# The first FFN's gate and product move to PSUM, preparation blocks are cut into four steps, and the first map loads change queue

## The chip, the cores and the metric

The kernel runs on one core of a Trainium2 chip. The core has TensorE (matmuls; PE, and PEld for its weight loads), VectorE (DVE), ScalarE (ACT), GpSimd (POOL) and SyncE (SP, which here only issues DMAs). SBUF is the on-chip memory of 128 partitions; PSUM is TensorE's output memory, in eight banks of 128 x 512 float32. The metric is the device time of one execution in microseconds (us); less is better.

## The reference

A decoder trunk of two layers over 512 positions of width 1024, all in float32. Layer 0 mixes positions by attention, layer 1 by a state-space recurrence (S5); each mixer is followed by a gated FFN with a causal convolution of width 3. Cut to the parts that matter here:

```python
def s5_ssm(h, w_in, a_re, a_im, log_dt, b_re, b_im, c_re, c_im, d_skip, w_glu, b_glu, w_o):
    lam_bar = jnp.exp(lam * dt)
    b_bar = ((lam_bar - 1) / lam)[..., None] * b_mat
    ...
def conv_ffn(h, w_up, conv_w, conv_b, w_down):
    up = h @ w_up
    up = lax.conv_general_dilated(up, conv_w[:, None, :], ...) + conv_b
    gate, val = jnp.split(up, 2, axis=-1)
    return (jax.nn.silu(gate) * val) @ w_down
...
    x = x + g1[:, None, :] * y
    h = modulate(rms_norm(x, norm_ffn[i]), sh2, sc2)
    x = x + g2[:, None, :] * conv_ffn(h, w_up[i], conv_w[i], conv_b[i], w_down[i])
```

The maps of the state-space layer (powers of `lam_bar`, `b_bar`, products with `c`) depend on weights alone. They are computed while the first FFN runs.

## The kernel before, in words

**Three matmuls for one.** Each float32 weight is split into a high part (ScalarE copy to a rounded type, L163) and a low part (VectorE subtraction, L164); the activations likewise. `mm3` then issues three matmuls, high by high, high by low, low by high (L169, L172, L173). Weights arrive by SP as 128 x 1024 tiles (`up_r`, `dn_r`, L161) into three raw buffers and five pairs of split buffers. `split_next` keeps the loads and splits ahead of use; `bg` puts rows of the conditioning matrix (`wg`, L195 and L196) in between.

**The FFN.** The 22 units of 128 hidden channels come in three groups of 8, 8 and 6 (`GROUPS`). A unit computes two up tiles (gate and value, each one PSUM bank of the six in pool `mm`; a second pool `aux` has two banks for statistics), and `unit_out` finishes it: `conv` for the gate (ScalarE L457, then two VectorE taps L459), Silu in place on ScalarE (L466), `conv` for the value, the product `gm` on VectorE (L469), and its split `gH` (ScalarE L473) and `gL` (VectorE L474). After each group the down projection adds that group's units into the residual: eight tiles `dn`, each over all units of the group. The first two tiles go over all but the last unit before the last unit is wanted. The first two units of an FFN, the head, are computed while the norm is still being applied.

**Order.** On ScalarE and VectorE, `follow` chains the FFN's instructions in the order written. Otherwise a scheduler orders each engine's instructions ahead of time from modelled durations; `keep_in_program_order` (in `held` and `pe_pin`) ties an instruction behind the one traced before it on its engine. Each engine, and SP's queue, then runs in that fixed order.

**The preparation.** `ssm_prep` is a generator. `pace` is called with 11.0 after each unit from the third on and with 5.4 after each down tile, and calls `step()` once for each `PACE` of credit; each call runs to the next `yield`. First come the exponentials and sines (VectorE, small), powers and rotation tables (`cmul`, six GpSimd instructions L870 to L875, stored by GpSimd's own DMA, L992). Then the tables' pool closes and eight blocks follow. A block computes `bl` (`cmul` of the loaded maps `lam` and `bt`), `cl` (six GpSimd instructions from `bc` and the powers) and `bd` (copies), stores `bl` to `sB` and `cl` to `sC`; `direct` makes sixteen matmuls `pk` from `bd` and `cl`, a ScalarE copy and a VectorE correction into `kz`, and eight stores to `sT`. `cl_out` and `direct` run one block late (`owe`). The loads `ball`, `lam`, `bt`, `bc` and all these stores were issued by SP (L1006, L1022, L1025), most of them through `held`. The state-space stage reads `sB`, `sR`, `sT` and `sC` back after the FFN.

Of the kernel before, what the change touches and what calls it, by code (L numbers as in the profile page):

```python
# [16 lines left out]
P = 128  # L17
T = 512
# [21 lines left out]
NIDLE = (7, 4, 4)  # L40
USTG = (6, 7)
BGU = 2
PACE = 12.0
NHOLD = 2
APIN = 7
FILL = (4, 7, 10, 14)
# [44 lines left out]
def _trunk(ctx, tc, I, out, tap):  # L91
# [47 lines left out]
    def follow(eng, fn):  # L139
        with tc.issue_after(line[eng].ins) if eng in line else ExitStack():  # L140
            line[eng] = fn()
        return line[eng]
# [281 lines left out]
    def ffn(l, R, prep=None, last=None, hook=lambda: None):  # L424
# [4 lines left out]
        with ExitStack() as fc:  # L429
# [33 lines left out]
            def unit_out(i, j, pss, nxt=lambda: None):  # L463
                cg = conv(i, 0, pss[0])
                nxt()
                follow("S", lambda: S.activation(cg, cg, AF.Silu))  # L466
                cv = conv(i, 1, pss[1])
                m = fp.tile([P, T], F32, tag="gm", bufs=1, name="gm")
                follow("V", lambda: V.tensor_tensor(m, cg, cv, ALU.mult))  # L469
                nxt()  # L470
                gh = fp.tile([P, T], F32R, tag=f"gH{j}", name=f"gH{i}")
                gl = fp.tile([P, T], F32R, tag=f"gL{j}", name=f"gL{i}")
                follow("S", lambda: S.activation(gh, m, AF.Copy))  # L473
                follow("V", lambda: V.tensor_tensor(gl, m, gh.bitcast(F32), ALU.subtract))  # L474
                return gh, gl
# [389 lines left out]
    def ssm_prep(fc):  # L865
# [3 lines left out]
        def cmul(orr, oi, ar, ai, br, bi, t1, t2, e=E):  # L869
            e.tensor_tensor(t1, ar, br, ALU.mult)  # L870
            e.tensor_tensor(t2, ai, bi, ALU.mult)
            e.tensor_tensor(orr, t1, t2, ALU.subtract)
            e.tensor_tensor(t1, ar, bi, ALU.mult)
            e.tensor_tensor(t2, ai, br, ALU.mult)
            e.tensor_tensor(oi, t1, t2, ALU.add)  # L875
# [4 lines left out]
        def gen():  # L880
# [29 lines left out]
            V.tensor_tensor(ph, are, dt, ALU.mult)  # L910
            expo(mag, ph)
            yield

            V.tensor_tensor(ph, aim, dt, ALU.mult)
            NA = 9
# [41 lines left out]
            V.tensor_tensor(fi, t1, t2, ALU.subtract)  # L957
            V.tensor_tensor(fi, fi, den, ALU.mult)
            yield

            lf = pt_.tile([P, 2, 8, NPAIR], F32, tag="lf", name="lf")
            lt1, lt2 = (pt_.tile([P, 8, NPAIR], F32, tag=g, name=g) for g in ("lt1", "lt2"))
            f0, f1 = (f.rearrange("p (o q) -> p o q", o=1).to_broadcast([P, 8, NPAIR]) for f in (fr, fi))
            cmul(lf[:, 0, ::-1, :], lf[:, 1, ::-1, :], pw[:, 0, :8, :], pw[:, 1, :8, :], f0, f1, lt1, lt2)
            yield

            def lf_out():
# [9 lines left out]
            for hb in range(2):  # L977
                ps_ = slice(hb * HP, (hb + 1) * HP)
                tb = pt_.tile([P, 2, HP, NC], F32, tag="tb", name="tb")
                tt = pt_.tile([P, 2, HP, 32], F32, tag="tt", name="tt")  # L980
                E.memset(tb[:, 0, :, 0:1], 1.0)
                E.memset(tb[:, 1, :, 0:1], 0.0)
                for q in range(6):
                    n = 1 << q
                    e0, e1 = bcast(co[:, 3 + q, ps_], n), bcast(si[:, 3 + q, ps_], n)
                    cmul(tb[:, 0, :, n:2 * n], tb[:, 1, :, n:2 * n], tb[:, 0, :, :n], tb[:, 1, :, :n], e0, e1, tt[:, 0, :, :n], tt[:, 1, :, :n])
                    if q > 3:
                        yield
                    if hb == 0 and q == 4:
                        lf_out()  # L990
                for ri in range(2):
                    G.dma_start(sR[hb * 4:(hb + 1) * 4, :, ri, :].rearrange("b p n -> p b n"), tb[:, ri].rearrange("p (b q) c -> p b (q c)", b=4))  # L992
# [10 lines left out]
            bb = pb.tile([P, 2, NPAIR, 16], F32, tag="bb", name="bb")  # L1003
            ball = pb.tile([P, 2, NPAIR, 16], F32, tag="bl", name="ball")
            for ri in range(2):
                SP.dma_start(ball[:, ri].rearrange("p a b -> p (a b)"), I[("b_re", "b_im")[ri]])  # L1006

            def v3(t):
                return t[:, :512].rearrange("p (q o) -> p q o", o=16)
# [3 lines left out]
            def direct(bi, bd, cl):  # L1013
                pk = bank(aux, f"pk{bi}")
                for ri in range(2):
                    for q in range(4):
                        pe_pin(PE.matmul(pk[q * 32:(q + 1) * 32, :P], bd[:, ri, q, :], cl[:, ri, q, 0:8, :].rearrange("p a h -> p (a h)"), start=ri == 0, stop=ri == 1))
                kz = kza[:, bi % 2, :]
                S.activation(kz[:, 112:], pk[:, :P], AF.Copy)
                V.scalar_tensor_tensor(kz[:, 112:128], delta, sm("d_skip", bi, 1), kz[:, 112:128], ALU.mult, ALU.add)  # L1020
                for j in range(8):
                    SP.dma_start(sT[bi].rearrange("(h j) g c -> j g h c", j=8)[j], kz[:, 112 - 16 * j:240 - 16 * j])  # L1022

            def held(out, in_):
                tc.keep_in_program_order(SP.dma_start(out, in_))  # L1025

            def load_bl(bi):
                lam = pb.tile([P, 2, 512], F32, tag="lam", name="lam")
                bt = pb.tile([P, 2, 512], F32, tag="bt", name="bt")
                cs = slice(bi * 512, (bi + 1) * 512)  # L1030
                for ri in range(2):
                    held(lam[:, ri, :], sL[ri, :, cs].rearrange("(o j) x -> o j x", o=1).to_broadcast([16, 8, 512]))
                    held(bt[:, ri, :], I[("b_reT", "b_imT")[ri]][:, cs].rearrange("h (o x) -> h o x", o=1).to_broadcast([16, 8, 512]))
                return lam, bt

            def cl_out(bi, cl):
                for ri in range(2):
                    for g2 in range(2):
                        held(sC[bi, ri * 64:ri * 64 + 64].rearrange("n (q g) c -> g n q c", g=2)[g2],
                             cl[g2 * 64:g2 * 64 + 64, ri, :, 1:, :].rearrange("n q a h -> n q (a h)"))  # L1040
# [3 lines left out]
            nxt = load_bl(0)  # L1044
            for bi in range(8):
                qs = slice(bi * 4, bi * 4 + 4)
                if owe:
                    cl_out(bi - 1, owe[2])
                bc = pb.tile([P, 2, 4, 16], F32, tag="bc", name="bc")
                for ri in range(2):  # L1050
                    held(bc[:, ri].rearrange("p a b -> p (a b)"), I[("c_re", "c_im")[ri]][:, bi * 64:(bi + 1) * 64])
                bl = pb.tile([P, 2, 512], F32, tag="bl", name="bl")
                lam, bt = nxt
                cmul(bl[:, 0], bl[:, 1], lam[:, 0], lam[:, 1], bt[:, 0], bt[:, 1], t1[:, :512], t2[:, :512])
                yield
                held(sB[bi].rearrange("p r n -> p (r n)"), bl.rearrange("p r n -> p (r n)"))
                if bi < 7:
                    nxt = load_bl(bi + 1)
                if owe:
                    direct(*owe)  # L1060
                cl = pb.tile([P, 2, 4, 9, 16], F32, tag="cl", name="cl")

                def v4(t):
# [16 lines left out]
                for g2 in range(2):  # L1080
                    rr = slice(g2 * 64, g2 * 64 + 64)
                    E.tensor_copy(bd[rr, :, :, g2 * 16:g2 * 16 + 16], bb[rr, :, qs, :])
                owe = bi, bd, cl
                yield
            cl_out(7, owe[2])
            direct(*owe)
            tc2.close()

        g = gen()
# [406 lines left out]
```

## Time and profile before

| what | value |
|---|---|
| three runs | 1194.74, 1194.81, 1198.65 us (median 1194.81) |
| profiled execution | 1194.65 us |
| its span, first to last instruction | 1192.7 us |
| mean granted TensorE clock | 0.991 |
| busy: PE, DVE, ACT, POOL | 1168.8, 885.8, 563.7, 270.4 us |
| first FFN, first up matmul to last down stage's begin | 268.1 to 616.0 us |
| second FFN, the same | 820.2 to 1148.7 us |

Lines such as `L474 DVE TENSOR_TENSOR gL<-gm,gH 128x512 ... x8 | 13.3, 1663 | 0.0` name a source line, an engine, an operation, what it writes and reads, and its count; then busy time in us and mean ns of one; then the engine's idle time just before and what ended it. A line of waits reads: who <- whom: us in total, times, longest. A line of the timeline begins with the start and the length in us. "Granted clock" is the share of TensorE's full clock that the chip allowed in a stretch.

### The profile page before, as it was taken

The numbers are of one execution on the slowest core, as the hardware profiler recorded it, in microseconds if no ns is written. First come the engines' busy times: TensorE is split into PE (matmuls) and PEld (weight loads), VectorE is DVE, ScalarE is ACT, GpSimd is POOL, SyncE is SP. The second block draws the span as 40 slices with busy tenths as digits, with TensorE's granted clock in tenths as the row PEclk, the third lists the DMA queues.
The fourth block names the chain that finished last, engine by engine and source line by source line (L and its number), as shares of the span: only waits on it lengthen the run. The fifth ranks groups of instructions, "written<-read, shape, count | busy, mean of one in ns | idle before, by whom it ended". The sixth has DMA issues, their size and how long they took to land.

```text
span 1192.7 us, 16459 instructions
## 1 busy us (share of the span) xinstructions
PE 1168.8 (98%) x6218; PEld 964.4 (81%) x6218; DVE 885.8 (74%) x1312; ACT 563.7 (47%) x893; POOL 270.4 (23%) x245
## 2 busy tenths in 40 slices
PE   8999999999999999989999999999999999999997
PEld 6887677699787878768889887879888888888887
DVE  6978988565999489888868598787598467744555
ACT  6756667456443134413336577646554134422443
POOL 1000000000298899998710000000000000000003
PEclk8999999999999999989999999999999999999999
DMA  8875653231348567778755598762166437442222
GB/s 301 316 262 165 203 179 109 90 121 54 89 142 273 177 215 222 207 233 294 247 153 182 182 322 288 246 224 77 53 216 225 124 118 188 153 124 71 83 76 71
DMA packets 92002, 211.00 MB, mean 177 GB/s; under 512 B 19602, under 2 KB 37906, under 8 KB 91923
## 3 DMA queue, kind: packets, MB, share of 16 engines
q1 hardware_dynamic: 83026, 205.76, 53.9%
q10 hardware_dynamic: 8320, 2.10, 0.8%
q0 software_dynamic: 576, 2.10, 0.5%
q8 instruction: 48, 0.79, 0.3%
q14 instruction: 32, 0.25, 0.1%
HBM read 188.68 MB, written 21.24 MB: 176 GB/s over the span
## 4 chain that ended last, share of the span: by engine, by line
PE 70%; POOL 8%; DVE 8%; DMA 7%; ACT 3%; issue 2%; SPq 1%; POOLq 0%; ACTq 0%; DVEq 0%
PE up L169 9%; PE up L172 9%; PE up L173 9%; PE dn L172 5%; PE dn L169 5%; PE dn L173 5%; PE o L772 2%; DVE ca L459 1%; PE t L754 1%; PE k L169 1%; PE q L169 1%; PE wo L169 1%; PE q L172 1%; PE q L173 1%; PE wo L173 1%
## 5 line engine op out<-in xcount | busy, mean ns | idle before, releaser
L173 PE MATMUL up<-hH,up_l 128*128 128x512 f32 x640 | 249.3, 390 | 1.1 <-DVE up_l L164 1.1
L169 PE MATMUL up<-hH,up_h 128*128 128x512 f32 x640 | 249.5, 390 | 0.0
L172 PE MATMUL up<-hL,up_h 128*128 128x512 f32 x640 | 249.3, 390 | 0.0
L459 DVE SCALAR_TENSOR_TENSOR ca<-up,small,ca 128x511 f32<-128x511 f32 (+1 forms) x176 | 131.4, 746 | 84.2 <-ACT ca L457 81.4
L196 DVE SCALAR_TENSOR_TENSOR wg<-wg,cact 128x1024 f32<-128x1024 f32 x96 | 122.8, 1294 | 40.1 <-DMA wg<-in_w_modT_dram 39.9
L172 PE MATMUL dn<-gL,dn_h 128*128 128x512 f32 (+1 forms) x394 | 145.9, 370 | 3.4 <-DVE gL L474 3.4
L169 PE MATMUL dn<-gH,dn_h 128*128 128x512 f32 (+1 forms) x394 | 146.3, 372 | 2.1 <-ACT gH L473 2.1
L173 PE MATMUL dn<-gH,dn_l 128*128 128x512 f32 (+1 forms) x394 | 145.7, 370 | 0.0
L173 PEld LDWEIGHTS up<-hH,up_l 128*128 128x128 f32 x640 | 120.1, 188 | 26.9 <-DVE up_l L164 2.0
L169 PEld LDWEIGHTS up<-hH,up_h 128*128 128x128 f32 x640 | 120.1, 188 | 26.0 <-issue 1.2
L172 PEld LDWEIGHTS up<-hL,up_h 128*128 128x128 f32 x640 | 120.1, 188 | 24.4
L1368 POOL TENSOR_SCALAR xa<-x,Anorm_out 128x256 f32<-128x256 f32 x7 | 5.7, 815 | 573.7 <-ACT dn_h L163 558.9
L163 ACT ACTIVATE up_h<-up_r 128x1024 fp32r<-128x1024 f32 x80 | 84.2, 1053 | 104.7 <-PE dn L172 48.0
L164 DVE TENSOR_TENSOR up_l<-up_r,up_h 128x1024 fp32r<-128x1024 f32 x80 | 121.9, 1524 | 10.1 <-ACT up_h L163 9.2
L457 ACT ACTIVATE ca<-up,small 128x512 f32<-128x512 f32 x88 | 67.7, 770 | 90.3 <-PE up L173 90.3
L172 PEld LDWEIGHTS dn<-gL,dn_h 128*128 128x128 f32 x394 | 75.1, 191 | 16.3 <-DVE gL L474 4.0
L169 PEld LDWEIGHTS dn<-gH,dn_h 128*128 128x128 f32 x394 | 75.0, 190 | 15.9 <-ACT gH L473 3.0
L173 PEld LDWEIGHTS dn<-gH,dn_l 128*128 128x128 f32 x394 | 75.0, 190 | 12.4
L353 DVE SCALAR_TENSOR_TENSOR x<-dn,mod,x 128x512 f32<-128x512 f32 (+1 forms) x55 | 37.3, 679 | 61.6 <-PE dn L173 61.6
L163 ACT ACTIVATE dn_h<-dn_r 128x1024 fp32r<-128x1024 f32 (+1 forms) x48 | 46.7, 981 | 55.9 <-PE dn L172 28.0
L466 ACT ACTIVATE ca<-ca 128x512 f32<-128x512 f32 x44 | 27.8, 632 | 91.7 <-DVE ca L459 89.9
L164 DVE TENSOR_TENSOR dn_l<-dn_r,dn_h 128x1024 fp32r<-128x1024 f32 (+1 forms) x48 | 62.8, 1308 | 8.3 <-ACT dn_h L163 8.1
(324 smaller groups left out, 2352.2 us busy)
## 6 DMA issues: line engine op xcount, KB each, us to landing
wg<-in_w_modT_dram SPq DMA_DIRECT2D x96, 512.0 KB
up_r<-in_w_up_dram SPq DMA_DIRECT2D x80, 512.0 KB
dn_r<-in_w_down_dram SPq DMA_DIRECT2D x32, 512.0 KB
wgs<-in_w_modT_dram SPq DMA_DIRECT2D x16, 512.0 KB
dn_r<-in_w_down_dram SPq DMA_DIRECT2D x16, 384.0 KB
wv_r<-in_w_v_dram SPq DMA_DIRECT2D x8, 512.0 KB
wk_r<-in_w_qk_dram SPq DMA_DIRECT2D x8, 512.0 KB
wq_r<-in_w_qk_dram SPq DMA_DIRECT2D x8, 512.0 KB
```

Of the source, the lines that this page charges most:

```text
L163: order("S", lambda: S.activation(wh[:, :n], raw[:, :n], AF.Copy))
L164: pin["split"] = order("V", lambda: V.tensor_tensor(wl[:, :n], raw[:, :n], wh[:, :n].bitcast(F32), ALU.subtract))
L169: ins = PE.matmul(ps, ah, bh, start=start, stop=False)
L172: PE.matmul(ps, ah, bl, start=False, stop=False)
L173: PE.matmul(ps, al, bh, start=False, stop=stop)
L196: mul = lambda: V.scalar_tensor_tensor(w, w, 1.0, cact, ALU.mult, ALU.mult, accum_out=raw[:, col:col + 1])
L353: add = lambda: V.scalar_tensor_tensor(xs, pv, gate, xs, ALU.mult, ALU.add)
L457: follow("S", lambda: S.activation(ca, ps, AF.Identity, bias=small[:, cb:cb + 1], scale=tapw[2]))
L459: follow("V", lambda: V.scalar_tensor_tensor(ca[:, q:], ps[:, :T - q], tapw[2 - q], ca[:, q:], ALU.mult, ALU.add))
L466: follow("S", lambda: S.activation(cg, cg, AF.Silu))
L754: ins = PE.transpose(pt[:, c:c + P], wts[pr][h2][i][:, j * P:(j + 1) * P], ident)
L772: ins = PE.matmul(po[pr][h2 * HD:(h2 + 1) * HD, j * P:], vn[:, j, hd:hd + HD], src, start=j == 0, stop=j == 3)
```

## The change

Four edits, all of them in the first FFN or in the preparation that runs beside it (`prep` is given for layer 0 alone).

1. `unit_out`: with `prep`, one PSUM bank `gm` a unit takes both the Silu's result and, in place, the product. Units 0 and 1 take it from `aux`, the others from `mm`. Before, the Silu was in place in SBUF and the product in an SBUF tile.
2. `PACE` is 6.0, not 12.0. The steps ahead of the blocks get a second, empty `yield`, so they keep their distance; a block has four steps: the product `bl`; the store of the block before's `cl`, its `direct` and the `bc` loads; `cl`, `bd` and half of the block before's `sT` stores; the store of `bl`, the next block's map loads and the other half of the `sT` stores.
3. The `sT` stores leave `direct`, become `t_out`, and go through `held`.
4. The two `ball` loads and the four map loads of block 0 are issued by GpSimd.

```diff
-PACE = 12.0
+PACE = 6.0
...
                 cg = conv(i, 0, pss[0])
                 nxt()
-                follow("S", lambda: S.activation(cg, cg, AF.Silu))
+
+                m = bank(aux if i < 2 else mm, "gm") if prep else fp.tile([P, T], F32, tag="gm", bufs=1, name="gm")
+                ga = m if prep else cg
+                follow("S", lambda: S.activation(ga, cg, AF.Silu))
                 cv = conv(i, 1, pss[1])
-                m = fp.tile([P, T], F32, tag="gm", bufs=1, name="gm")
-                follow("V", lambda: V.tensor_tensor(m, cg, cv, ALU.mult))
+                follow("V", lambda: V.tensor_tensor(m, ga, cv, ALU.mult))
...
             expo(mag, ph)
             yield
+            yield
...
             for ri in range(2):
-                SP.dma_start(ball[:, ri].rearrange("p a b -> p (a b)"), I[("b_re", "b_im")[ri]])
+                G.dma_start(ball[:, ri].rearrange("p a b -> p (a b)"), I[("b_re", "b_im")[ri]])
...
-                for j in range(8):
-                    SP.dma_start(sT[bi].rearrange("(h j) g c -> j g h c", j=8)[j], kz[:, 112 - 16 * j:240 - 16 * j])
+
+            def t_out(bi, js):
+                kz = kza[:, bi % 2, :]
+                for j in js:
+                    held(sT[bi].rearrange("(h j) g c -> j g h c", j=8)[j], kz[:, 112 - 16 * j:240 - 16 * j])
...
             def load_bl(bi):
+                put = held if bi else G.dma_start
...
-                    held(lam[:, ri, :], sL[ri, :, cs].rearrange("(o j) x -> o j x", o=1).to_broadcast([16, 8, 512]))
-                    held(bt[:, ri, :], I[("b_reT", "b_imT")[ri]][:, cs].rearrange("h (o x) -> h o x", o=1).to_broadcast([16, 8, 512]))
+                    put(lam[:, ri, :], sL[ri, :, cs].rearrange("(o j) x -> o j x", o=1).to_broadcast([16, 8, 512]))
+                    put(bt[:, ri, :], I[("b_reT", "b_imT")[ri]][:, cs].rearrange("h (o x) -> h o x", o=1).to_broadcast([16, 8, 512]))
...
             for bi in range(8):
                 qs = slice(bi * 4, bi * 4 + 4)
-                if owe:
-                    cl_out(bi - 1, owe[2])
-                bc = pb.tile([P, 2, 4, 16], F32, tag="bc", name="bc")
-                for ri in range(2):
-                    held(bc[:, ri].rearrange("p a b -> p (a b)"), I[("c_re", "c_im")[ri]][:, bi * 64:(bi + 1) * 64])
                 bl = pb.tile([P, 2, 512], F32, tag="bl", name="bl")
                 lam, bt = nxt
                 cmul(bl[:, 0], bl[:, 1], lam[:, 0], lam[:, 1], bt[:, 0], bt[:, 1], t1[:, :512], t2[:, :512])
                 yield
-                held(sB[bi].rearrange("p r n -> p (r n)"), bl.rearrange("p r n -> p (r n)"))
-                if bi < 7:
-                    nxt = load_bl(bi + 1)
                 if owe:
+                    cl_out(bi - 1, owe[2])
                     direct(*owe)
+                bc = pb.tile([P, 2, 4, 16], F32, tag="bc", name="bc")
+                for ri in range(2):
+                    held(bc[:, ri].rearrange("p a b -> p (a b)"), I[("c_re", "c_im")[ri]][:, bi * 64:(bi + 1) * 64])
+                yield
                 cl = pb.tile([P, 2, 4, 9, 16], F32, tag="cl", name="cl")
...
+                if owe:
+                    t_out(bi - 1, range(4))
                 owe = bi, bd, cl
+                yield
+                held(sB[bi].rearrange("p r n -> p (r n)"), bl.rearrange("p r n -> p (r n)"))
+                if bi < 7:
+                    nxt = load_bl(bi + 1)
+                if bi:
+                    t_out(bi - 1, range(4, 8))
                 yield
             cl_out(7, owe[2])
             direct(*owe)
+            t_out(7, range(8))
```

More of the change, by code (lines that the diff above doesn't have):

```diff
@@ L988, in gen @@
                         yield
+                        yield
                     if hb == 0 and q == 4:
@@ L1055, in gen @@
                 yield
-                held(sB[bi].rearrange("p r n -> p (r n)"), bl.rearrange("p r n -> p (r n)"))
-                if bi < 7:
-                    nxt = load_bl(bi + 1)
                 if owe:
+                    cl_out(bi - 1, owe[2])
                     direct(*owe)
+                bc = pb.tile([P, 2, 4, 16], F32, tag="bc", name="bc")
+                for ri in range(2):
+                    held(bc[:, ri].rearrange("p a b -> p (a b)"), I[("c_re", "c_im")[ri]][:, bi * 64:(bi + 1) * 64])
+                yield
                 cl = pb.tile([P, 2, 4, 9, 16], F32, tag="cl", name="cl")
@@ L1082, in gen @@
                     E.tensor_copy(bd[rr, :, :, g2 * 16:g2 * 16 + 16], bb[rr, :, qs, :])
+                if owe:
+                    t_out(bi - 1, range(4))
                 owe = bi, bd, cl
+                yield
+                held(sB[bi].rearrange("p r n -> p (r n)"), bl.rearrange("p r n -> p (r n)"))
[3 more added lines that the diff above has]
+                    t_out(bi - 1, range(4, 8))
                 yield
```

## The prediction

> **What bounds the kernel now.** I read the page first, then busy time by stretch, then TensorE's waits, then the instructions around each wait. The page says where the floor is.
>
> ```profile
> PE 1168.8 (98%) x6218; PEld 964.4 (81%) x6218; DVE 885.8 (74%) x1312; ACT 563.7 (47%) x893; POOL 270.4 (23%) x245
> ```
>
> TensorE is busy for 98% of the span, so no engine's total can shrink the time; only what TensorE loses can. The two FFNs are the same code on the same sizes, but only the first carries the state-space preparation, so the second is a ruler for the first. Below, busy time by stretch: first-group up, its down, second-group up, its down, third-group up, for layer 0 and then for layer 1. Columns: stretch, length, busy of PE, PEld, DVE, ACT, POOL, granted clock, DMA share and GB/s.
>
> ```profile
> 268.10:359.00 90.90, 90.00 (x469) 76.77 (x467) 76.89 (x175) 47.31 (x71) 37.67 (x57) 1.00 0.32 95
> 359.00:406.50 47.50, 45.80 (x195) 37.15 (x194) 33.96 (x38) 12.92 (x15) 37.38 (x46) 0.96 0.63 207
> 406.50:496.60 90.10, 89.85 (x434) 72.88 (x433) 78.18 (x69) 33.93 (x47) 86.92 (x60) 1.00 0.72 224
> 496.60:548.20 51.60, 47.75 (x225) 37.85 (x224) 39.02 (x37) 11.26 (x14) 49.99 (x33) 0.93 0.81 258
> 548.20:616.00 67.80, 67.80 (x337) 54.95 (x337) 57.76 (x60) 26.73 (x38) 42.48 (x26) 1.00 0.76 232
> 820.20:909.40 89.20, 89.20 (x465) 76.41 (x464) 70.38 (x114) 48.97 (x72) 0.00 (x0) 1.00 0.41 131
> 909.40:952.90 43.50, 43.50 (x193) 36.03 (x192) 22.66 (x26) 11.15 (x12) 0.00 (x0) 1.00 0.53 169
> 952.90:1039.90 87.00, 87.00 (x385) 72.06 (x384) 62.76 (x87) 35.29 (x45) 0.00 (x0) 1.00 0.56 152
> 1039.90:1083.50 43.60, 43.60 (x194) 36.08 (x194) 18.72 (x20) 10.63 (x11) 0.00 (x0) 1.00 0.38 119
> 1083.50:1148.70 65.20, 65.20 (x289) 54.01 (x288) 35.38 (x44) 25.30 (x33) 0.00 (x0) 1.00 0.26 74
> ...
> L1017 PE MATMUL pk<-cl,bd x128: 272/273/423, 439.2 to 604.8; 128*32 128x128 f32 x128
> ...
> 268.10:616.00 347.90, 0.60 (x4) 0.50 (x4) 0.58 (x1) 0.99 0.62 195
> ```
>
> Layer 0 is longer by 1.7, 4.0, 3.1, 8.0 and 2.6 us, 19.4 in all. Part of that is TensorE's own preparation work: eight groups of sixteen `pk` matmuls (the tile's row) and four `ptl` transposes of 0.60 us (the last row, busy time of that tile alone). Three `pk` groups fall in the third up stretch, which has no idle time, so one costs 2.6/3 = 0.87 us. Three more fall in the second up stretch and two in its down. That is 6.9 + 0.6 = 7.5 us of work; 19.4 - 7.5 = **11.9 us is loss**: 1.1 in the first up, 4.0 in the first down, 0.5 in the second up, 6.3 in the second down. The waits of TensorE and the clock tell how it is lost.
>
> ```profile
> PE dn L172 <- DVE gL L474: 3.4, 2, 2.7
> PE dn L169 <- ACT gH L473: 2.1, 2, 1.1
> PE up L173 <- DVE up_l L164: 1.1, 2, 0.9
> ...
> 368.70:375.30 6.60, 4.90 (x14) 3.64 (x14) 6.60 (x10) 3.69 (x4) 6.21 (x8) 0.74 0.79 241
> 506.20:515.30 9.10, 5.25 (x26) 3.32 (x26) 8.13 (x8) 2.75 (x3) 8.93 (x5) 0.62 0.70 215
> ```
>
> In each of the first two down stages TensorE reaches the product of the group's last unit before `gH` and `gL` are made: 1.0 + 0.7 us idle in the first, 1.1 + 2.7 in the second. After each wait the granted clock falls (0.74 and 0.62 over the two stretches), which makes 4.0 us out of 1.7 and 6.3 out of 3.8.
>
> **The change part by part.** *Gate and product in PSUM (22 units).* No instruction is added; Silu now writes a PSUM bank, the product reads bank and SBUF and writes the bank, and `gL` reads bank and SBUF. The rows are VectorE by form, first from 406 to 548 us with GpSimd running, then from 820 to 1000 without it.
>
> ```profile
> L474 DVE TENSOR_TENSOR gL<-gm,gH 128x512 fp32r<-128x512 f32 x8 | 13.3, 1663 | 0.0
> L459 DVE SCALAR_TENSOR_TENSOR ca<-up,small,ca 128x511 f32<-128x511 f32 x16 | 11.8, 738 | 0.0
> L469 DVE TENSOR_TENSOR gm<-ca,ca 128x512 f32<-128x512 f32 x8 | 9.9, 1244 | 0.2
> L164 DVE TENSOR_TENSOR up_l<-up_r,up_h 128x1024 fp32r<-128x1024 f32 x16 | 33.4, 2090 | 5.7 <-ACT up_h L163 5.7
> ...
> L164 DVE TENSOR_TENSOR up_l<-up_r,up_h 128x1024 fp32r<-128x1024 f32 x24 | 29.3, 1219 | 0.7 <-ACT up_h L163 0.2
> L459 DVE SCALAR_TENSOR_TENSOR ca<-up,small,ca 128x511 f32<-128x511 f32 x24 | 18.0, 748 | 24.6 <-ACT ca L457 24.6
> L469 DVE TENSOR_TENSOR gm<-ca,ca 128x512 f32<-128x512 f32 x12 | 8.3, 692 | 0.4
> L474 DVE TENSOR_TENSOR gL<-gm,gH 128x512 fp32r<-128x512 f32 x11 | 7.5, 686 | 1.4 <-ACT gH L473 1.4
> ```
>
> With GpSimd running, every operation on two SBUF tensors is stretched (`gL` 686 to 1663 ns, `gm` 692 to 1244, `up_l` 1219 to 2090); the convolution tap, one PSUM and one SBUF input, is not (748 and 738). So I take 0.75 us for both new operations. No row has VectorE writing PSUM: the ends are 0.69 us (nothing but the size counts) and today's 1.24 and 1.66 (nothing gained; a loss is excluded by nothing but the tap, which is nearest). Gain per unit 0.49 + 0.91 = 1.4 us of VectorE, about 11 us over the second group's eight units, worth only what the two waits return. Units 0 and 1 take their bank from the statistics' pool: the statistics and their broadcast have been read by then, since the head's operands are made from them, so this costs nothing; were it not free, ScalarE would stand at the Silu with the next unit's copies behind it.
>
> [...]
>
> First down stage. The queue of VectorE there, the ScalarE row that makes the last `gH`, and ScalarE's copy out of PSUM by form:
>
> ```profile
> 350.62 1.53 DVE L474 TENSOR_TENSOR gL<-gm,gH 128x512 fp32r<-128x512 f32 x1
> 353.76 1.52 DVE L459 SCALAR_TENSOR_TENSOR ca<-up,small,ca 128x511 f32<-128x511 f32 x2
> 358.68 2.20 DVE L469 TENSOR_TENSOR gm<-ca,ca 128x512 f32<-128x512 f32 x1
> ...
> 369.08 0.63 ACT L473 ACTIVATE gH<-gm 128x512 fp32r<-128x512 f32 x1 [1.05 <-DVE gm L469]
> ...
> L457 ACT ACTIVATE ca<-up,small 128x512 f32<-128x512 f32 x16 | 12.2, 762 | 0.0
> ```
>
> VectorE is busy for all 6.60 us around the wait, so what is cut earlier arrives there. The `gL` and the `gm` shown give back 0.78 + 1.45 = 2.2 us, more than the 1.7 that TensorE waited. ScalarE's `gH` takes 0.63 us from SBUF; its copy out of PSUM, with two pointers, 0.76, so 0.13 us each for `gH` and Silu is the worst, and they eat 0.3 of the 0.5 to spare. The whole **4.0 us** goes. Next late is then the `dn_l` split of the tile after, in the same queue.
>
> *Preparation blocks in four steps.* The second down stage, VectorE and ScalarE:
>
> ```profile
> 502.10 1.52 DVE L164 TENSOR_TENSOR dn_l<-dn_r,dn_h 128x1024 fp32r<-128x1024 f32 x1 [3.65 <-ACT dn_h L163]
> 505.09 1.59 DVE L469 TENSOR_TENSOR gm<-ca,ca 128x512 f32<-128x512 f32 x1
> 508.82 1.75 DVE L474 TENSOR_TENSOR gL<-gm,gH 128x512 fp32r<-128x512 f32 x1
> ...
> 501.00 1.06 ACT L163 ACTIVATE dn_h<-dn_r 128x1024 fp32r<-128x1024 f32 x1 [5.73 <-DMA dn_r<-in_w_down_dram]
> ...
> SPq L1025 <- POOL bl L875: 28.8, 7, 6.5
> SPq L1006 <- DMA sR<-tb: 18.0, 2, 15.6
> ...
> 489.98 0.33 SPq L1025 DMA_DIRECT2D sB<-bl  x1
> 493.01 1.01 SPq L161 DMA_DIRECT2D dn_r<-in_w_down_dram  x2
> ```
>
> PSUM alone gives 0.84 (`gm`) + 1.00 (`gL`) = 1.84 of the 3.8 us idle. The rest hangs on a load: ScalarE stands 5.73 us for `dn_r`, and the last unit's Silu and product stand behind it. That load was issued at 493.01, behind `sB` and four map loads; `sB` was held until GpSimd had finished `bl`, one of seven such holds of 28.8 us together, 6.5 at most. In the new order `sB` comes three steps of 6 us behind its product instead of one of 12, with the store of the previous `cl` behind the next product, and the eight `sT` stores in two lots a step or two behind their matmuls. If the 6.5 us go, `dn_h` can be some 5.7 us earlier and the 3.65 us of VectorE idle with it: 1.84 + 3.65 = 5.5, more than 3.8. Only 2.0 of the 3.65 are needed. I take **5.3 of 6.3 us**, keeping 1.0 for a load that is still somewhat late. What can be late next: GpSimd's next product, whose maps are now loaded one step ahead of it; TensorE meets that only in `pk`, after the product and `cl`.
>
> The count of steps and the pace balance: 24 steps of 12 were 288 credits, 47 of 6 are 282. The first content comes half a block (6 us) earlier, into the third unit. Its small VectorE operations surround the `up_l` wait of the first up stretch (1.1 us lost); it may go or double. I take 0, ends -1.1 and +1.1.
>
> *First loads by GpSimd.* Two `ball` and four map loads leave SP, where they were held up to 15.6 us for `sR` to land, with weights behind them. TensorE lost 0.5 us in the stretch that follows; I take **0.5 us** back. GpSimd pays for six issues:
>
> ```profile
> L992 POOL DMA_DIRECT2D sR<-tb x4 | 3.3, 816 | 0.6 <-POOL tb L875 0.6
> ```
>
> 6 x 0.82 = 4.9 us on its queue, hidden because the last `pk` (604.8) stands 11 us ahead of the third up's end (616.0) and only later stages read the stores.
>
> *Sum*: 4.0 + 5.3 + 0.5 = 9.8 us. The profiled execution took 1194.65 us (span 1192.7 and 1.95 around it), 0.16 under the median of 1194.81: 1194.65 - 9.8 = **1184.9 us**. All 11.9 us back would be 1182.8.
>
> **The rivals.** *The load stays late, PSUM works.* Then the second down keeps 2.0 us idle and its share of slow clock: 6.3 x 2.0/3.8 = 3.3 stays, gain 4.0 + 3.0 + 0.5 = 7.5, 1187.2 us. For it: GpSimd itself is what SP waits for, and it is busy 49.99 of 51.60 us there.
>
> *The queue waits in a new place.* The `sT` stores are now held in order and need `pk`, a ScalarE copy and a VectorE operation; a weight load behind one of them stalls ScalarE as `dn_r` did. If one wait of the second down's size returns, 4.0 + 0.5 or less is kept: 1190 to 1194.5 us, no change. For it: seven holds at present, and an order that was timed for instructions of other length. Against: each store is now further behind what it waits for.
>
> *Slower: the banks run out.* Each unit now takes three of six banks, so the banks of a unit come round after two units, not three. The up tile of unit 6 ended three tiles before 358.4, at 5.2 us each: 342.8; its taps (the row at 353.76) ended at 355.3, a lag of 12.5 us, and the bank is wanted after 3 x 5.2 = 15.6. From a lag of 15.6 on TensorE waits in the middle of up. One us over, on six units, at the 4.0/1.7 that an idle us costs with the clock: 6 x 2.35 = 14 us, against a gain then of at most 5: 1204 us. Against it: the new lengths shorten the lag.
>
> [...]
>
> **How the numbers follow.** Forecast 0.46 (1182.8 to 1187), late load 0.16, new place 0.23, starved issues 0.04, banks 0.11. A measurement of this kernel can tell about 0.5%, 6 us. Faster by more: 0.46 + 0.16 = 0.62; within: 0.27; slower: 0.11. The range goes from 1181.8 (all the loss back, and 1 us that another order in later stages may give) to 1194.8 (the whole of the new-place case), leaving out the banks and little else; the likeliest case alone spans 1182.8 to 1187.
>
> **What would show it.** `gm` and `gL` in layer 0 near 0.75 us throughout; `up_l` still near 2; the waits of `dn` on `gH` and `gL` gone and the clock 1.00 in both down stretches, which then last 43.5 and 45.3 us; SP's hold on `bl` well under 28.8 us. Wrong if VectorE writing PSUM is slow, if a wait on `up` or `dn` appears that ends with a tap (banks), or if an order shifted after 616 us moves the state-space stage, which I hold unchanged.

## The result, and the profile after

The changed kernel took 1199.11 us (median of 20 runs, 1196.94 to 1204.29) against 1194.28 us for the kernel before (20 runs). The ratio is **1.0046, with a 95% interval of 1.0033 to 1.0058**: a little slower, and outside the range of the prediction. The profiled execution has a span of 1196.0 us and a mean clock of 0.991. Busy time of the engines, kernel after:

```profile
PE 1167.7 (98%) x6218; PEld 965.4 (81%) x6218; DVE 853.3 (71%) x1312; ACT 564.4 (47%) x893; POOL 254.5 (21%) x251
```

VectorE has 32.5 us less to do and GpSimd 15.9, TensorE the same work as before. The time is not lost to more work.

First the view that the prediction used as its ruler: busy time by stretch, first FFN of the kernel after (first up, its down, second up, its down, third up; columns as before).

```profile
269.70:360.60 90.90, 90.28 (x469) 76.71 (x468) 76.68 (x176) 49.88 (x75) 37.96 (x59) 1.00 0.36 108
360.60:404.10 43.50, 43.50 (x194) 36.03 (x192) 35.67 (x43) 11.23 (x12) 35.55 (x45) 1.00 0.75 244
404.10:511.60 107.50, 92.44 (x450) 74.32 (x448) 59.03 (x65) 36.03 (x49) 93.89 (x76) 0.92 0.69 204
511.60:556.80 45.20, 45.20 (x229) 36.64 (x225) 36.75 (x39) 10.67 (x13) 38.50 (x25) 1.00 0.86 270
556.80:623.90 67.10, 67.10 (x324) 54.75 (x321) 45.71 (x55) 25.59 (x36) 32.60 (x22) 1.00 0.65 197
```

Against the rows of before (90.9, 47.5, 90.1, 51.6 and 67.8 us) the two downs gained 4.0 and 6.4 us and both run at clock 1.00, as forecast. The second up lost 17.4 us, and here lies the whole surprise: PE was busy for only 92.44 of 107.50 us. The five stages sum to 354.2 us against 347.9, 6.3 more; the medians differ by 4.8. TensorE's waits of this stretch of the program, kernel after (who <- whom: us in total, times, longest):

```profile
PE pk L1023 <- POOL cl L1083: 11.8, 1, 11.8
PE pk L1023 <- POOL cl L1086: 3.3, 1, 3.3
PE up L173 <- DVE up_l L164: 0.3, 1, 0.3
PE up L169 <- DVE ca L459: 0.3, 1, 0.3
```

All waits on `gH` and `gL` are gone. In their place stands one that the kernel before did not have: the first `pk` matmuls wait 15.1 us for GpSimd's `cl`. The instructions around it, on TensorE and then on GpSimd, kernel after:

```profile
414.75 0.39 PE L173 MATMUL up<-hH,up_l 128*128 128x512 f32 x1
426.92 0.65 PE L1023 MATMUL pk<-cl,bd 128*32 128x128 f32 x8 [11.78 <-POOL cl L1083]
430.86 0.66 PE L1023 MATMUL pk<-cl,bd 128*32 128x128 f32 x8 [3.28 <-POOL cl L1086]
431.44 0.80 PE L169 MATMUL up<-hH,up_h 128*128 128x512 f32 x1
```

```profile
425.47 1.39 POOL L1083 TENSOR_TENSOR cl<-t,t 128x576 f32<-128x576 f32 x1
...
429.41 1.40 POOL L1086 TENSOR_TENSOR cl<-t,t 128x576 f32<-128x576 f32 x1
```

TensorE stands in front of `pk` from 415.1 us, one unit into the second up. GpSimd finishes the two halves of `cl` at 426.86 and 430.81. The same two events in the kernel before, one row of each engine:

```profile
434.41 2.29 POOL L1078 TENSOR_TENSOR cl<-t,t 128x576 f32<-128x576 f32 x1
...
439.21 0.64 PE L1017 MATMUL pk<-cl,bd 128*32 128x128 f32 x16
```

There `cl` was ready at 436.70 and `pk` came at 439.21, three units into the up: 2.5 us to spare. So GpSimd is not late in the changed kernel, it is 5.9 us *earlier*. It is TensorE that comes to `pk` too early, by two units (48 up matmuls ahead of it in this stretch instead of 144).

The credits of the pace give the reason. Six units of 11.0 and eight down tiles of 5.4 make 109.2 at the begin of the second up; 120.2 stand after unit 8, 131.2 after unit 9 and 142.2 after unit 10. Block 0's `direct` was in the 11th step of 12, due at 132, and so came after unit 10. In the new division it is in the 20th step of 6, due at 120, and comes after unit 8. Twelve credits are about one unit; 131.2 against 132 made it two.

A second wait hides behind the first. SP's holds on `bl` and on `kz`, and SP's queue around the first of them, kernel after:

```profile
SPq L1034 <- POOL bl L877: 29.4, 2, 27.2
...
SPq L1034 <- DVE kz L1026: 2.1, 2, 1.7
```

```profile
395.34 0.33 SPq L195 DMA_DIRECT2D wg<-in_w_modT_dram  x1
422.96 0.33 SPq L1034 DMA_DIRECT2D sB<-bl  x1
...
426.20 0.53 SPq L161 DMA_DIRECT2D up_r<-in_w_up_dram  x1
```

Where seven holds of 6.5 us at most stood, there is one of 27.2. SP, no longer held by `ball`, ran on to block 0's `sB` at 395.7 and stood there until GpSimd had made `bl`; the next weight was issued at 426.20. TensorE was waiting for `cl` at the time, so this cost nothing more, as long as the other wait stood. Two runs below bear out that the moved loads brought it: with only edit 1 and the loads still on SP (e4) the longest hold on `bl` is 5.6 us, and with only the loads moved (e10) it is 25.4.

### The profile page after: what moved, and what is told of

The parts are those of the page before. It is cut to its first block, busy times and chain, and to the rows that moved or that the text cites. A ratio compares the mean times of both kernels' runs of the same rounds, so it can differ in the third digit from the quotient of the medians.

```text
span 1196.0 us, 16497 instructions
## 1 busy us (share of the span) xinstructions
PE 1167.7 (98%) x6218; PEld 965.4 (81%) x6218; DVE 853.3 (71%) x1312; ACT 564.4 (47%) x893; POOL 254.5 (21%) x251
## 4 chain that ended last, share of the span: by engine, by line
PE 82%; POOL 9%; DVE 5%; ACT 2%; issue 1%; DMA 1%; POOLq 0%; ACTq 0%; DVEq 0%
PE up L169 12%; PE up L172 11%; PE up L173 11%; PE dn L169 5%; PE dn L173 5%; PE dn L172 5%; PE o L774 2%; PE u L172 1%; PE t L756 1%; PE u L169 1%; PE u L173 1%; PE wo L169 1%; PE wo L173 1%; PE wo L172 1%; PE k L169 1%
## 5 line engine op out<-in xcount | busy, mean ns | idle before, releaser
L169 PEld LDWEIGHTS up<-hH,up_h 128*128 128x128 f32 x640 | 120.5, 188 | 26.7 <-issue 2.1
L164 DVE TENSOR_TENSOR up_l<-up_r,up_h 128x1024 fp32r<-128x1024 f32 x80 | 112.7, 1408 | 1.9 <-ACT up_h L163 1.0
L163 ACT ACTIVATE dn_h<-dn_r 128x1024 fp32r<-128x1024 f32 (+1 forms) x48 | 46.8, 982 | 44.9 <-PE dn L172 38.1
```

The source lines that it names most:

```text
L163: order("S", lambda: S.activation(wh[:, :n], raw[:, :n], AF.Copy))
L164: pin["split"] = order("V", lambda: V.tensor_tensor(wl[:, :n], raw[:, :n], wh[:, :n].bitcast(F32), ALU.subtract))
L169: ins = PE.matmul(ps, ah, bh, start=start, stop=False)
```

## Experiments

The medians of the kernel before lay between 1191.79 and 1194.69 us in the four sets of runs, so each kernel is given by its ratio to the runs beside it. Outside the first FFN, profiled executions of one and the same code differ by some us (the state-space stage from its first `u` matmul to the `wos` matmuls took 119 to 123 us over all kernels, before among them); the stages of the FFN are therefore read from the trace. Where an expectation counts up matmuls ahead of `pk`, the count begins 142 matmuls ahead of the second up.

**e1, two steps later.** Block 0's `pk`, with all of its `sT` stores, behind the store of block 1's `sB`; the other blocks unchanged.

```diff
-                    direct(*owe)
+                    if bi > 1:
+                        direct(*owe)
...
-                owe = bi, bd, cl
+                late, owe = owe, (bi, bd, cl)
...
+                if bi == 1:
+                    direct(*late)
```

> The changed kernel with block 0's sixteen pk matmuls (and its sT stores) written two steps later, at 132 credits, so that they follow unit 10 on TensorE as in the kernel before, not unit 8. Theory (place): the 15.1 us of TensorE waiting for GpSimd's cl of block 0 is the whole loss, and all other parts of the change gain: cl ends near 431 us, TensorE reaches pk near 436, no wait; the second up stretch falls from 107.5 to about 90 us, the kernel from 1199.1 to about 1181.7, 12.6 us under the kernel before. Rival (GpSimd late because of its own six DMA issues): the same here, as the place hides the lateness. Rival (the wait only moves, since TensorE's time was never the limit): 1190 or more, with a new wait of the same kind at pk1 or later.

Measured: 1187.65 us, ratio 0.9939 (0.9919 to 0.9960), 6.0 us above the time that the theory gave. The `pk` wait is gone and the second up takes 97.2 us, not 107.5. That the change is now faster than the kernel before shows the first wait as the main cause (10.3 of the 17.4 us). But 97.2 is not 90: the second wait has come into the open. Waits of TensorE, of SP, and ScalarE's row ahead of it, e1:

```profile
PE up L169 <- ACT up_h L163: 2.6, 1, 2.6
PE up L173 <- DVE up_l L164: 1.6, 2, 1.2
```

```profile
SPq L1034 <- POOL bl L877: 40.2, 5, 27.4
```

```profile
433.16 1.06 ACT L163 ACTIVATE up_h<-up_r 128x1024 fp32r<-128x1024 f32 x1 [17.02 <-DMA up_r<-in_w_up_dram]
```

SP's hold of 27.4 us keeps a weight back, ScalarE waits 17.02 us for it, and TensorE waits for 4.2 us of that.

**e2, one step later.** Only the `pk` of block 0, behind the making of block 1's `cl`.

> As e1, but one step later instead of two: pk of block 0 follows unit 9. Place: TensorE reaches it near 425.3, cl ends near 431, so it waits 5 to 6 us and loses 1 to 2 us of clock behind: 1188 to 1189.5 us, between the changed kernel and e1. A rival in which the wait is not a matter of place has no reason for a value in between.

Measured: 1189.38 us, ratio 0.9959 (0.9944 to 0.9975). TensorE waits 1.1 and 3.5 us at `pk` (`cl` of block 0), two units into the up; the second up takes 97.2 us again. One unit of room is too little by 4.6 us. The time is in the expected range, but it does not part e2 from e1: the intervals overlap and the second up is equally long. SP's longest hold on `bl` is 27.4 us here too, and as in the changed kernel no late weight shows beside the wait at `pk`.

**e3, the first loads back on SP.** The kernel after, with the two `ball` and the four map loads of block 0 issued by SP as before.

```diff
-                G.dma_start(ball[:, ri].rearrange("p a b -> p (a b)"), I[("b_re", "b_im")[ri]])
+                SP.dma_start(ball[:, ri].rearrange("p a b -> p (a b)"), I[("b_re", "b_im")[ri]])
...
-                put = held if bi else G.dma_start
+                put = held
```

> The changed kernel with ball and block 0's map loads issued by SP again; pk of block 0 still follows unit 8. Place: GpSimd ends cl at 427 to 434 all the same, the wait stays 12 us or more, 1197 to 1201 us. Rival (GpSimd's own issues made it late): cl ends some 5 us or more earlier, the wait falls under 10 us, under 1193 us. SP also holds the weights behind the loads again, up to 0.5 us.

**e4, PSUM alone.** The kernel before, with edit 1 only.

> The kernel before with the gate and product in PSUM and nothing else changed; pk of block 0 follows unit 10. Prediction's terms: the first down's 4.0 us gone, of the second down's 6.3 us 3.0 gone (the load stays late), so 1187 us, 7 under the kernel before. Rival (VectorE's shorter operations were never what TensorE waited for): 1192 or more. gm and gL 0.68 to 0.70 us.

Measured: e3 1200.49 us, ratio 1.0058 (1.0040 to 1.0076); e4 1196.31 us, ratio 1.0003 (0.9985 to 1.0021). Both lost in a place that the prediction did not have: the *first* down, 57.6 and 57.4 us. TensorE's waits in e3, then TensorE's wait, SP's hold and SP's queue in e4:

```profile
PE dn L173 <- DVE dn_l L164: 12.5, 1, 12.5
PE pk L1023 <- POOL cl L1086: 2.8, 1, 2.8
```

```profile
PE dn L173 <- DVE dn_l L164: 9.4, 2, 6.3
```

```profile
SPq L1008 <- DMA sR<-tb: 24.4, 2, 22.1
```

```profile
369.19 0.34 SPq L161 DMA_DIRECT2D dn_r<-in_w_down_dram  x1
394.16 0.33 SPq L1008 DMA_DIRECT2D ball<-in_b_re_dram  x1
...
396.27 0.53 SPq L161 DMA_DIRECT2D dn_r<-in_w_down_dram  x1
```

e3's time was as expected, but by luck: the wait at `pk` is 2.8 us, not 12 or more, because TensorE had lost its time in the first down and came to `pk` only at 426.6. Its `cl` was ready at 423.12 and 429.79, 3.7 and 1.0 us sooner than in the changed kernel, not the 5 of the rival. e4 missed its 1187 us by 9.

With edit 1 alone the fixed order of SP's queue comes out otherwise: `ball` now stands ahead of the group's last down weight. In the kernel before, the last `dn_r` of that stage was issued at 373.42 and three up weights after it, before SP met `ball`. Here SP stands at `ball` for 22.1 us, until `sR` has landed, and the weight of the last down tile leaves at 396.27. Block 0's `sB` has moved up as well: with edit 1 and no pause 17 issues of `up_r` stand ahead of it (e1 to e4, e7 and the changed kernel), without edit 1 there are 19 (the kernel before, e8, e10, e11). So moving the loads to GpSimd is worth some 14 us of the first down *beside* edit 1 (57.6 against 43.5), where the prediction had 0.5 in all. Most of it goes again in the second up: 12.7 us from e3 to the changed kernel, where TensorE now comes to `pk` ahead of `cl`, and 6.1 from e4 to e7, where SP now reaches `sB` early. And e4's second down takes 45.2 us at clock 1.00: gate and product in PSUM cure it alone. VectorE's last `gL` ahead of it, and the matmul that takes it, e4:

```profile
512.98 0.68 DVE L476 TENSOR_TENSOR gL<-gm,gH 128x512 fp32r<-128x512 f32 x1
...
517.94 0.39 PE L172 MATMUL dn<-gL,dn_h 128*128 128x512 f32 x1
```

That `gL` is ready 5.5 us after the stage begins (at 508.2), 4.3 us before TensorE wants it; in the kernel before it came 14.0 us after the begin.

**e5, a pause of three steps.** The kernel after, with three empty steps ahead of block 0's store to `sB`, so that this store and all that follows come 18 credits later.

```diff
                 owe = bi, bd, cl
                 yield
+                if bi == 0:
+                    for q in range(3):
+                        yield
                 held(sB[bi].rearrange("p r n -> p (r n)"), bl.rearrange("p r n -> p (r n)"))
```

> The changed kernel with three empty steps (18 credits) ahead of block 0's store of bl, which also moves that block's next map loads and its pk matmuls: sB stands behind up_11 in SP's queue, not behind up_10, and pk follows unit 10. Theory now: two waits for GpSimd make the loss, pk on TensorE (15.1 us) and sB on SP (27 us), behind which the weights of units 10 to 12 stand (7 us of TensorE in e1). Expected: SP's hold on bl under 10 us, no wait at pk, the second up stretch 89.6 to 91 us, 1181 to 1183 us, ratio near 0.989. Rival (the splits themselves or the DMA rate limit units 10 to 12): the second up stays at 95 us or more, 1187.

Measured: 1182.88 us (6 runs), ratio **0.9914 (0.9887 to 0.9942)**, faster than both kernels. Waits of TensorE and SP, then the stretch of the second up and the sum over the five, e5:

```profile
PE pk L1023 <- POOL cl L1086: 1.3, 1, 1.3
```

```profile
SPq L1034 <- POOL bl L877: 22.0, 3, 15.3
```

```profile
402.80:493.90 91.10, 89.75 (x433) 72.91 (x432) 60.12 (x65) 35.04 (x48) 84.54 (x68) 1.00 0.66 200
...
sum 338.50, PE 336.52 PEld 277.27 DVE 258.69 ACT 133.20 POOL 244.67; mean PE 67.30 PEld 55.45 DVE 51.74 ACT 26.64 POOL 48.93
```

Both waits fell together, and the first FFN is 9.4 us shorter than in the kernel before. SP's longest hold is 15.3 us, more than the 10 expected, but no wait of TensorE for a weight above 0.3 us is left. Against the changed kernel no instruction was added or taken away: it is the place alone.

**e6, the stores of block 0 off SP.** e1, with block 0's `sB` and block 1's map loads issued by GpSimd.

> As e1, with block 0's store of bl and block 1's four map loads issued by GpSimd, which makes bl itself, so that SP never waits for it there; nothing else is moved. Queue theory: the hold of 27 us and TensorE's wait for weights at 434 us both go, the second up stretch 89.6 to 91 us, 1181 to 1183 us; GpSimd pays about 3 us for five issues. Rival (weights late for another reason than SP's queue): 97 us as in e1, 1187.5.

Measured: 1190.83 us, ratio 0.9977 (0.9958 to 0.9996); not what was expected. SP's and TensorE's waits, e6:

```profile
SPq L1034 <- POOL cl L1084: 34.7, 1, 34.7
```

```profile
PE up L169 <- ACT up_h L163: 4.8, 1, 4.8
```

SP ran past the place of `sB` to the next held store, block 0's `sC`, and stood there for 34.7 us. Taking one early wait off a queue in fixed order uncovers the next one; e5 moves them all.

**e7, two steps.** The kernel before with edits 1 and 4: blocks still in two steps of 12.

> The kernel before with the gate and product in PSUM and the first loads issued by GpSimd, blocks in two steps of 12 as before; pk of block 0 follows unit 10, sB stands behind up_10. If the four steps bring nothing: first down 43.5, second down 45.2 as in e4, the hold of sB about 27 us and the second up near 97 us as in e1, so 1187 to 1188. If the four steps were what cured the second down (the prediction's term): second down 48 us or more, 1190.

Measured: 1189.82 us, ratio 0.9967 (0.9949 to 0.9986), 1.8 us above the 1188 expected at most. First down 43.6, second down 45.2, second up 95.7 us with 4.2 us of waits on `up_h` and `up_l` behind a hold on `bl` of 26.7 us. Both downs are cured without the four steps.

**e8, no PSUM; e10, GpSimd's loads alone; e11, four steps alone.** The remaining combinations of the edits.

> The changed kernel without PSUM: Silu and product in SBUF as before; pk of block 0 follows unit 8. GpSimd is again slowed by VectorE's product and gL, cl of block 0 ends 434 to 440 us and TensorE waits for it 15 us or more; the first down keeps its 4 us, the second its 3 to 6: 1200 to 1210 us. If PSUM were not what cured the two downs, they last 43.5 and 45.2 and it equals the changed kernel, 1199.

> The kernel before with only the six first loads moved to GpSimd; gate and product in SBUF, steps of 12. Theory (with these loads off SP the queue runs on to the first sB and stands there for bl, as in e7; the two down stages keep their waits, since VectorE's product and split are as slow as before): first down 46 to 47.5 us, second up 93 to 97, second down 50 to 51.6, the first FFN 350 to 354 us against 347.9, the time 1196 to 1201 us. Rival (the loads were what held the down weights, as e4's 57.4 us suggested, so moving them helps by itself): second up 90, first down 43.5 to 45, 1189 to 1192 us.

> The kernel before with only the blocks in four steps of 6 (and the sT stores held in order); first loads on SP, gate and product in SBUF. Theory (the first pk is placed after unit 8 while cl of block 0 ends at the pace of the kernel before, 436.7 us, so TensorE waits there for cl as in the kernel after): a wait of TensorE's pk on cl of 12 to 22 us, second up 104 to 118 us, second down 45 to 49 because VectorE catches up during the wait, the time 1202 to 1215 us. Rival (the four steps are harmless by themselves, and pk is late only together with the other edits): pk wait under 3 us, second up 90 to 92, 1189 to 1196 us.

All eight combinations (stages of the first FFN in us; ratio to before). "Four steps" are edits 2 and 3 together:

| PSUM | four steps | loads by GpSimd | kernel | up, down, up, down, up | sum | ratio (95%) |
|---|---|---|---|---|---|---|
| no | no | no | before | 90.9, 47.5, 90.1, 51.6, 67.8 | 347.9 | 1 |
| yes | no | no | e4 | 90.8, 57.4, 89.6, 45.2, 67.8 | 350.8 | 1.0003 (0.9985-1.0021) |
| no | yes | no | e11 | 99.2, 43.5, 102.0, 45.2, 67.2 | 357.1 | 1.0086 (1.0055-1.0116) |
| no | no | yes | e10 | 90.8, 44.9, 92.6, 56.2, 67.8 | 352.3 | 1.0015 (0.9995-1.0034) |
| yes | yes | no | e3 | 91.0, 57.6, 94.8, 45.2, 67.2 | 355.8 | 1.0058 (1.0040-1.0076) |
| yes | no | yes | e7 | 90.8, 43.6, 95.7, 45.2, 67.8 | 343.1 | 0.9967 (0.9949-0.9986) |
| no | yes | yes | e8 | 99.5, 43.5, 102.9, 45.2, 67.1 | 358.2 | 1.0081 (1.0056-1.0106) |
| yes | yes | yes | after | 90.9, 43.5, 107.5, 45.2, 67.1 | 354.2 | 1.0046 (1.0033-1.0058) |

e8 took 1202.85 us, as expected, but both signs missed: the `pk` wait is 10.7 us, not 15 or more, and the downs lost nothing. e10 took 1195.81 us. Its theory was right on the sum alone (352.3 us): the first down of 44.9 is what the rival had, the second up of 92.6 is just short of 93, and the second down of 56.2 is longer than in any other kernel. TensorE waits there 4.9 us for `gH` and 2.4 for `gL`; VectorE is busy for 280.3 us of the five stages, nearly as long as before (285.8; e4 260.4). In e11 the theory's direction holds (1202.98 us), and its sizes for the second up (104 us or more) and the wait (12 or more) were too high.

Each pair that differs in the four steps alone is longer with them: by 9.2 us (nothing else), 5.0 (PSUM), 5.9 (loads), 11.1 (both). With two steps the other two edits help only together: PSUM adds 2.9 us alone and takes away 9.2 beside the loads. In e8 and e11, without PSUM, the four steps bring a second wait of the same kind in the first up. TensorE's waits in e11:

```profile
PE pk L1021 <- POOL cl L1081: 6.8, 1, 6.8
PE ptl L973 <- POOL lf L875: 6.0, 1, 6.0
PE pk L1021 <- POOL cl L1084: 1.7, 1, 1.7
```

The `ptl` transposes also come earlier (349.11 us in e11, 358.61 before), and GpSimd's `lf` is not ready. In the kernel after it is: GpSimd's last `lf`, first in the kernel before, then after:

```profile
351.56 1.18 POOL L875 TENSOR_TENSOR lf<-lt,lt 128x256 f32<-128x256 f32 x1
```

```profile
344.22 0.73 POOL L877 TENSOR_TENSOR lf<-lt,lt 128x256 f32<-128x256 f32 x1
```

That is 7.8 us earlier on GpSimd, and with PSUM left out (e8) the wait is back (6.0 us at `ptl`, `lf` ready at 353.47), so it is edit 1 that lets GpSimd run ahead. e11's `pk` wait, 8.5 us, is below the 12 expected: TensorE had already stood 6.0 us at `ptl`, and `cl` was ready at 433.87, not at 436.7. The downs of e8 and e11 are short without PSUM. In both, TensorE had stood in the up stage just ahead (6.0 us at `ptl` in the first; at `pk` in the second 10.7 us in e8, 8.5 in e11), time in which VectorE could catch up; no kernel has the four steps without PSUM and without these waits, so what the four steps alone do to the downs stays open.

**e9, a pause of four steps.** e5 with one more empty step.

> Block 0's store to sB, and with it every later step, comes one step later than in e5, so the first pk comes after unit 11 (334 up matmuls of the second group ahead of it, not 286). Theory (the place of the first pk and of the first sB against GpSimd's end is all that was wrong): the 1.35 us pk wait of e5 goes, the second up lasts 89.5 to 91.0 us, SP's hold on bl stays at 22 us or less, the time is 1181 to 1183 us, equal to e5 within 0.2%. Rival (lateness is paid at the other end: the last blocks' pk slide into the third up and past it): third up or the stage behind it grows by 1 us or more and the time is 1184 to 1188 us.

Measured: 1184.84 us (6 runs), ratio 0.9925 (0.9900 to 0.9951): not to be told from e5 by time, and 1.8 us above the 1183 expected at most, in the range of its rival. The rival's sign is not there in the third up (67.8 us, as before); the stretch from there to the second FFN took 203.8 us against 201.8 in e5, but 199 to 205 over all kernels, so the rest stays open. In the trace the `pk` wait is gone and no loss is left in the five stages. SP's hold, then the second up and the sum, e9:

```profile
SPq L1034 <- POOL bl L877: 9.8, 3, 4.7
```

```profile
401.10:490.50 89.40, 89.40 (x433) 72.87 (x432) 57.95 (x64) 35.71 (x48) 81.86 (x64) 1.00 0.69 204
...
sum 336.80, PE 336.18 PEld 277.19 DVE 254.90 ACT 133.62 POOL 244.34; mean PE 67.24 PEld 55.44 DVE 50.98 ACT 26.72 POOL 48.87
```

**e12, two steps and a pause.** e7 with one empty step of 12 ahead of block 0's `sB`.

> e7 (gate and product in PSUM, first loads by GpSimd, blocks in two steps of 12) with one empty step of 12 ahead of block 0's store to sB: the same places of pk as in e9, but two steps to a block. Theory (placing the first sB and pk behind GpSimd is what the kernel needs, and four steps bring nothing of their own): SP's longest hold on bl falls from 26.7 to 16 us or less, TensorE loses under 1.5 us in the second up, which lasts 89.5 to 91.5 us, the first FFN 336.5 to 339.5 us, the time 1181 to 1185 us, as e5 and e9. Rival (with two steps SP's later holds on bl stay long, 48.4 us in all in e7, and reach TensorE through a late weight; the four steps are needed to cure that): second up or second down keeps 2 to 5 us of loss on up_h, up_l or dn_h, 1186 to 1190 us.

Measured: 1188.84 us, ratio 0.9969 (0.9949 to 0.9990), second up 93.4 us. Waits of SP and TensorE, e12:

```profile
SPq L1027 <- POOL bl L877: 49.0, 7, 28.7
```

```profile
PE up L169 <- ACT up_h L163: 1.4, 1, 1.4
```

The expectation missed, and the time is in the range of the rival. `pk` now comes four units into the up and does not wait, but `sB` still stands right behind the weight issued at 395.03, and SP is held for 28.7 us. In the code `sB` is 24 credits behind its product here, in e9 42; in SP's queue it stands behind 18 issues of `up_r`. In e7 there are 17 and the longest hold is 26.7 us, in e5 20 and 15.3, in e9 22 and 4.7. So the length of SP's hold goes with the place of `sB`, not of `pk`, which has the same place in e12 and e9. Whether two steps with `sB` as late as in e9 would do as well, or the four steps are needed for it, was not tried.

## Why the prediction was wrong

- **Both downs** (4.0 and 5.3 us taken): right, 4.0 and 6.4 measured, clock 1.00. `gm` and `gL` came to 695 and 679 ns, below the 0.75 us taken; `up_l` to 1752, from 2090. VectorE by form from 406 to 548 us, kernel after:

```profile
L164 DVE TENSOR_TENSOR up_l<-up_r,up_h 128x1024 fp32r<-128x1024 f32 x14 | 24.5, 1752 | 0.0
...
L471 DVE TENSOR_TENSOR gm<-gm,ca 128x512 f32<-128x512 f32 x8 | 5.6, 695 | 0.1
L476 DVE TENSOR_TENSOR gL<-gm,gH 128x512 fp32r<-128x512 f32 x8 | 5.4, 679 | 0.0
```

- **How the second down was shared out: wrong.** The prediction gave PSUM 1.84 us of its idle time and the four steps the rest, by way of an earlier `dn_r`. e4 and e7 have 45.2 us without the four steps. The rows of one wait were added up as if the queue ahead of it had not changed; with eight units' work cut by 1.5 us each, VectorE has the last `gL` ready 8.5 us earlier in the stage (e4: 5.5 against 14.0 us after its begin), far more than the 1.84 taken.
- **The step that failed: "Preparation blocks in four steps".** It named the danger ("TensorE meets that only in `pk`, after the product and `cl`") and took it as nothing. It checked the *last* `pk` (604.8) against the end of the third up, and never worked out after which unit the *first* one comes, though pace and step counts were all there. By the rows, two units earlier are 2 x 10.9 = 21.8 us plus 2.4 for the earlier begin of the stage; against that stood 2.5 us to spare and whatever GpSimd would gain (5.9). The sum of this, 15.8 us, is close to what was measured at `pk` (15.1), before the slow clock behind it (0.50 for 3.2 us). The 2.4 and the 5.9 are from the trace after; the rows of before alone give 21.8 - 2.5 = 19.3 us.
- **SP's hold on `bl`**, "well under 28.8 us": 29.4, nearly all of it in one piece. The distance from product to store was counted in steps, which count TensorE's progress; GpSimd's, which makes `bl`, was not looked at. And the hold on `ball` (15.6), which was to go, had kept SP from reaching `sB` early (e4 and e10).
- **First loads by GpSimd** (0.5 us): mis-sized. Beside PSUM they save about 14 us in the first down (e3) and 7.7 of the five stages (e4 against e7), since the order that came with edit 1 puts `ball` ahead of a down weight; without PSUM they cost 4.4 (e10). That shift of the order could not be read from the trace before; it was a cost without a row and got no range of its own.
- **Rivals.** A queue waiting in a new place was the right family, but pictured at the `sT` stores, whose holds on `kz` came to 2.1 us, and priced too low by taking one wait of the old size. Starved issues (the chance of 0.04, for GpSimd's six issues taking longer than 0.82 us each): refuted, first and last of the six in the kernel after:

```profile
402.78 0.56 POOL L1012 DMA_DIRECT2D ball<-in_b_re_dram  x1 [2.51 <-DMA sR<-tb]
...
405.44 0.58 POOL L1044 DMA_DIRECT2D bt<-in_b_imT_dram  x1
```

Six issues of 0.55 to 0.58 us each, below the 0.82 taken. Banks: refuted, the only wait on a tap is 0.3 us.

With the first `pk` and `sB` in place (e5) the kernel gains 0.86%, about 10 us, close to the 9.8 forecast; the forecast was in effect that of a kernel whose first block comes three steps later. That the two agree so well is partly luck: the downs give 10.4 us, not 9.3, and the second up loses 1.0 where 0.5 was to be gained.

## What to carry to other kernels

When steps are cut finer or moved on a credit scale, work out for the *first* of each kind after which unit it now falls, and set it against the finishing time of the engine that feeds it; the rows of both are in the trace before, and rounding to whole units can double the shift. On a queue with a fixed order, a hold that is removed lets the queue run on to the next early wait (e10: 25.4 us on `bl`; e6: 34.7 us on `cl`), so place the whole group of waiting instructions later, not one of them. Where a scheduler plans the order ahead of time, an edit that only moves tiles to another memory can come with another order of a queue that it does not touch (e4: 22.1 us at `ball`), and parts tested one at a time need not add up.

## What the hardware showed beyond the forecast

- VectorE's product takes about as long into PSUM: 695 ns for 128 x 512 with one input in PSUM, 692 with both in SBUF and GpSimd silent; `gL` with one input in PSUM took 679 ns, 686 with both in SBUF. The tap, from which the prediction took its 0.75 us, is at 748 ns, 56 above the product, but it is another operation, so the difference need not be that of the source.
- GpSimd was faster with the same edit: with edit 1 alone (e4) its 222 instructions of the five stages were busy for 240.4 us, against 254.4 for as many before. VectorE's operations became shorter there too (260.4 us busy against 285.8). In the kernel after, `gm` (1244 to 695 ns) and GpSimd's last `lf` (1.18 to 0.73 us, ready 7.8 us earlier) go the same way. What ties the lengths on the two engines together, these traces do not show.
- After the 15.1 us of waiting the granted clock is a half for 3.2 us. Two stretches of the kernel after, columns as before:

```profile
431.40:434.60 3.20, 3.20 (x12) 2.49 (x8) 0.75 (x1) 1.22 (x2) 3.12 (x3) 0.50 0.88 218
434.60:438.00 3.40, 3.40 (x16) 2.83 (x15) 3.20 (x4) 0.60 (x1) 3.32 (x3) 0.99 0.89 349
```

  In the next 3.4 us it is 0.99. In all, the wait of 15.1 us cost 17.0 (107.5 against 87.0 in the second FFN plus four `pk` groups of 0.87).
